# Expert stages of a two-layer mixture-of-experts backbone: TensorE's work in a written order, and weight tiles that hold two neighbouring rows per partition

## The chip, the cores and the metric

The kernel runs on one core of a Trainium2 chip, as one launch. Its metric is the device time of that launch in microseconds. A core has a matrix engine (TensorE, PE in the profile), a vector engine (VectorE, DVE), a scalar engine (ScalarE, ACT), a general engine (GpSimd, POOL), an engine that here only issues transfers (SyncE, SP) and 16 DMA engines that move data between the device memory and the on-chip memory. All work on their own and wait for one another through semaphores.

## What is computed

Two layers work on 512 latent tokens and 256 context tokens of 1024 features, all in fp32. Each layer is a sequence mixer (an mLSTM in layer 0, a retention in layer 1) followed by a mixture of 16 experts, in which every expert chooses its own tokens. The mixture is the part that the change is about:

```python
def expert_choice_ffn(h, router, w_gate, w_up, w_down):
    bn, t, _ = h.shape
    cap = CAPACITY_FACTOR * t // N_EXPERTS          # 64 latent or 32 context tokens
    aff = jax.nn.softmax(h @ router, axis=-1)
    gate, idx = lax.top_k(jnp.swapaxes(aff, 1, 2), cap)
    xs = h[bidx, idx]
    hid = jax.nn.silu(einsum('becd,edf->becf', xs, w_gate)) * einsum('becd,edf->becf', xs, w_up)
    y = einsum('becf,efd->becd', hid, w_down) * gate[..., None]
    return jnp.zeros_like(h).at[bidx, idx].add(y)
...
for i in range(DEPTH):                              # 2 layers
    ...                                             # mixer, added to x (and to ctx in layer 0)
    h_lat = modulate(rmsnorm(x, norm_ffn_g[i]), mod_l[3], mod_l[4])
    x = x + mod_l[5] * expert_choice_ffn(h_lat, moe_router[i], moe_w_gate[i], moe_w_up[i], moe_w_down[i])
    if not last:                                    # layer 0 alone: the context stream too
        h_ctx = modulate(rmsnorm(ctx, norm_ffn_g[i]), mod_c[3], mod_c[4])
        ctx = ctx + mod_c[5] * expert_choice_ffn(h_ctx, moe_router[i], ...)
return rmsnorm(x, final_norm_g)
```

Every expert has three matrices of 1024 x 1024 fp32 (4.19 MB each), so a layer reads 16 x 12.58 MB = 201.3 MB of expert weights, each used once.

## The kernel before

**Weights.** `load` (L1165) fetches the matrices on SP's queue in tiles of 1.05 MB: 128 partitions x 2 x 1024 fp32, that is 256 rows of a matrix, of which partition p holds row p and row p + 128. An expert has 12 tiles, in the order that `order` gives: four of gate, four of up, four of down. The tiles rotate through a fixed number of slots on the chip (`slot`; about 19 in layer 0 and 14 in layer 1). A load is issued when the last matmul that read its slot is done, so SP often stands and waits for PE.

**Layer 0.** An expert of the loop at the end of `moe` has 64 latent tokens (LAT in the code) and 32 context tokens (CTX). `prod` (L1276, its matmuls at L1282) makes a product: for each of 8 tiles of 128 features it puts the tokens as the stationary operand into a group of columns of PE and moves a piece of a weight row past them. The products are `gl` (gate, latent: 32 matmul records in the trace, 64 x 512), `ul` (up, latent), `cg` (gate and then up of the context: 64 records of 32 x 256 each, two halves of one accumulator) and `y` (down, of both streams, in the accumulators y0 and y1). Between them stand transposes: `xp` (L1243) turns the gathered token rows of the next expert into the stationary form, `hp` (L1433) does so with the hidden rows. ACT makes silu of the gate product (`hid`, L1425), DVE multiplies it by the up product (L1427), ACT copies `hp` into `hT` (L1435). DVE also scales the transposed tokens (`xs`, L1253 and L1255). GpSimd gathers tokens and adds results through indirect transfers.

**Layer 1.** Only latent tokens are left. Tokens are picked by matmuls with a 0/1 matrix for two experts at a time: `pick` (DVE, L1221), `xr` (8 matmuls of 128 x 512 for each half of the features, L1235), `rows` (ACT copy, L1238), `xp` (L1247), `xs`. After every odd expert the results of two experts are put back into the latent rows: `put_back` splits them into `bh` and `bl` (L296, L297), 16 matmuls `back` (L1313) spread them over the tokens, and DVE adds each 128 x 512 piece into x (L1316). The piece's accumulator `back` has two buffers. Expert 15 has a path of its own (`final_gain`, `finish`), in an order written by hand.

**What sets the order.** Outside that last expert a scheduler of the compiler orders the instructions of all engines, PE's too: the code gives the dependences, and the scheduler moves pieces of `gl`, `cg`, `ul`, `y`, `xr` and `back` between one another. Within `with tc.manual_schedule(engines=PE)` PE's instructions stand as the code is written.

## Time and profile before

| | |
|---|---|
| median of 3 runs | 1977.88 us (1977.67 to 1979.93) |
| the profiled execution | 1974.15 us |
| its span in the profile | 1972.4 us |
| mean granted clock of PE | 0.986 of full speed |
| PE busy | 1850.9 us, 94% of the span |
| DVE, ACT, POOL busy | 37%, 22%, 14% of the span |
| read from device memory | 544.13 MB |

The span is the time from the first to the last instruction in the profile; 1.75 us of the execution lie around it. The steady part of the expert loop of layer 0 lies between 533 and 1017 us, that of layer 1 between 1499 and 1921 us; together they are 906 us, 46% of the span. The rest are the two mixers, the routing, and the ends of the stages.

### The profile page before, as it was taken

The page shows a single profiled execution, that of the slowest core. Times are in us where ns is not written, and L with a number is a line of the kernel's source. Part 1 is how long each engine was busy: PE and PEld are TensorE (multiplying, and loading weights), DVE is VectorE, ACT ScalarE, POOL GpSimd, SP SyncE. Part 2 cuts the span into 40 slices and gives each one's busy share as a digit, 9 for nine tenths or more (in the row PEclk, how much of TensorE's full clock was granted, in tenths as well). Part 3 has the DMA queues.
Part 4 walks back from the last instruction along what each step waited for, and adds up shares of the span by engine and source line. Part 5 has one row for each costly group of instructions (what it writes and reads, how often), then busy time and mean ns, then how long its engine had stood idle before and what let it go on. Part 6 is the DMA issues. An engine that isn't in the chain of part 4 may idle for free. (4 is left out here: it accounts for less than half of the span.)

```text
span 1972.4 us, 27775 instructions
## 1 busy us (share of the span) xinstructions
PE 1850.9 (94%) x11091; PEld 1012.6 (51%) x11091; DVE 730.2 (37%) x1739; ACT 426.8 (22%) x839; POOL 279.8 (14%) x340
## 2 busy tenths in 40 slices
PE   7999988999999999999998999999979999989997
PEld 2765766787344443333334777788754333333332
DVE  3544567546111110110104677355551322222223
ACT  3532355432000000000004522322411000000001
POOL 1111133301211121120011124144000000000001
PEclk9999999999999999999999999999979999999999
DMA  8567776764999999999984588354559999999992
GB/s 285 205 209 268 253 207 196 230 228 144 333 393 375 391 383 384 383 382 393 401 319 126 182 279 276 112 173 150 208 208 395 415 416 414 415 414 414 416 413 86
DMA packets 218258, 585.42 MB, mean 297 GB/s; under 512 B 17674, under 2 KB 69618, under 8 KB 213010
## 3 DMA queue, kind: packets, MB, share of 16 engines
q1 hardware_dynamic: 209840, 570.72, 77.6%
q0 software_dynamic: 6912, 12.71, 3.2%
q8 instruction: 88, 1.44, 0.3%
q10 hardware_dynamic: 1378, 0.23, 0.1%
q14 instruction: 40, 0.33, 0.0%
HBM read 544.13 MB, written 39.47 MB: 296 GB/s over the span
## 5 line engine op out<-in xcount | busy, mean ns | idle before, releaser
L1282 PE MATMUL y<-wslot,hT 128*32 128x256 f32 (+1 forms) x2016 | 291.1, 488 | 9.8 <-ACT hT L1435 9.6
L1282 PE MATMUL gl<-wslot,xs 128*64 128x512 f32 x1024 | 260.3, 610 | 0.8 <-DVE xs L1255 0.8
L1282 PE MATMUL ul<-wslot,xs 128*64 128x512 f32 x1024 | 239.3, 596 | 0.0
L290 PE MATMUL acc<-whi,hT_hi 128*128 128x512 f32 x544 | 223.2, 411 | 4.8 <-ACT hT_hi L360 3.1
L291 PE MATMUL acc<-wlo,hT_hi 128*128 128x512 f32 x544 | 217.6, 400 | 0.3 <-POOL wlo L297 0.3
L292 PE MATMUL acc<-whi,hT_lo 128*128 128x512 f32 x544 | 217.3, 399 | 0.2 <-DVE hT_lo L361 0.2
L1427 DVE TENSOR_TENSOR hid<-hid,ul 128x512 f32<-128x512 f32 x32 | 22.0, 688 | 463.5 <-PE ul L1282 463.5
L1282 PEld LDWEIGHTS y<-wslot,hT 128*32 128x32 f32 (+1 forms) x2016 | 100.2, 123 | 178.1 <-issue 137.3
L1282 PEld LDWEIGHTS ul<-wslot,xs 128*64 128x64 f32 x1024 | 72.2, 137 | 140.8 <-issue 136.2
L1282 PEld LDWEIGHTS gl<-wslot,xs 128*64 128x64 f32 x1024 | 69.4, 138 | 135.5 <-issue 131.1
L290 PEld LDWEIGHTS acc<-whi,hT_hi 128*128 128x128 f32 x544 | 102.8, 189 | 39.4 <-issue 9.8
L1282 PE MATMUL cg<-wslot,xs 128*32 128x256 f32 x1920 | 118.9, 382 | 0.5 <-ACT hid L1425 0.5
L292 PEld LDWEIGHTS acc<-whi,hT_lo 128*128 128x128 f32 x544 | 102.8, 189 | 28.5 <-issue 4.9
L291 PEld LDWEIGHTS acc<-wlo,hT_hi 128*128 128x128 f32 x544 | 103.2, 190 | 23.7 <-issue 2.4
L1425 ACT ACTIVATE hid<-gl 128x512 f32<-128x512 f32 x32 | 19.1, 597 | 439.6 <-PE gl L1282 439.6
L297 DVE TENSOR_TENSOR wlo<-wslot,whi 128x512 fp32r<-128x512 f32 x108 | 80.6, 762 | 56.1 <-ACT whi L296 55.8
L1282 PEld LDWEIGHTS cg<-wslot,xs 128*32 128x32 f32 x1920 | 56.5, 109 | 84.1 <-issue 51.1
L296 ACT ACTIVATE whi<-wslot 128x512 fp32r<-128x512 f32 x112 | 69.4, 630 | 99.2 <-PE acc L292 98.2
L1435 ACT ACTIVATE hT<-hp 128x512 f32<-128x512 f32 (+1 forms) x48 | 23.7, 524 | 297.4 <-PE hp L1433 297.4
L1387 POOL TENSOR_TENSOR wslot<-x,wslot 128x512 f32<-128x512 f32 x4 | 5.0, 1271 | 493.2 <-DVE x L1330 491.6
L290 PE MATMUL po<-woh,yh 128*128 128x512 f32 x160 | 64.5, 403 | 3.2 <-ACT yh L923 3.2
L1449 DVE SCALAR_TENSOR_TENSOR o<-y,gcol,M 128x512 f32<-128x512 f32 (+1 forms) x32 | 19.8, 617 | 125.8 <-PE y L1282 125.8
(440 smaller groups left out, 2449.9 us busy)
## 6 DMA issues: line engine op xcount, KB each, us to landing
wslot<-in_moe_w_up_dram SPq DMA_DIRECT2D x128, 1024.0 KB
wslot<-in_moe_w_gate_dram SPq DMA_DIRECT2D x128, 1024.0 KB
wslot<-in_moe_w_down_dram SPq DMA_DIRECT2D x124, 1024.0 KB
wslot<-in_ada_w_dram SPq DMA_DIRECT2D x40, 1024.0 KB
wslot<-in_ret_w_in_dram SPq DMA_DIRECT2D x16, 1024.0 KB
wslot<-in_mlstm_w_in_dram SPq DMA_DIRECT2D x12, 1024.0 KB
wslot<-in_ada_w_dram SPq DMA_DIRECT2D x16, 512.0 KB
E<-rows_d SPq DMA_DIRECT2D x24, 256.0 KB
```

Source lines behind the costliest of these rows:

```text
L290: nc.tensor.matmul(o, lh, rh, start=first, stop=False)
L291: nc.tensor.matmul(o, lh, rl, start=False, stop=False)
L292: nc.tensor.matmul(o, ll, rh, start=False, stop=last)
L296: nc.scalar.activation(wh, w, AF.Copy)
L297: eng.tensor_tensor(wl, w, wh.bitcast(F32), op=OP.subtract)
L1282: mm = nc.tensor.matmul(o[cw * q:cw * q + cw, :], stat(k), w(k)[:, qn * n:(qn + 1) * n], start=(k == 0), stop=(k == 7), tile_position=(0, ...
L1387: nc.gpsimd.tensor_tensor(O[:, lo], R.X[t][:, lo], fg[:, lo], op=OP.mult)
L1425: nc.scalar.activation(HID[v], o, AF.Silu)
L1427: nc.vector.tensor_tensor(HID[v], HID[v], o, op=OP.mult)
L1435: LATE["act"] = nc.scalar.activation(HT[v], p, AF.Copy)
L1449: LATE["dve"] = nc.vector.scalar_tensor_tensor(r, o, TOP[v][2][:, e:e + 1], M5[v], op0=OP.mult, op1=OP.mult)
```

## The change

Three things are changed together.

1. A weight tile holds two neighbouring rows of the matrix in each partition (rows 2p and 2p + 1 of its 256), which lie in one piece of 8 KB in device memory; before, they were two pieces of 4 KB. The down matrix of the very last expert comes in pieces of 2 KB as before. Sizes, number and order of the loads stay.
2. So the feature that a partition holds is another, and whatever meets a weight tile on the feature axis is brought into that order: either the transposes of it read every second column, or the operation that writes it writes its elements in pairs 128 apart (`paired`, `pairs_of`). This touches the modulation vectors (a new tile `vcp`, filled by three loads `VP`), the router, the normalised rows, and `hid`, which ACT and DVE now write in that pattern in every expert.
3. PE's order in the expert loops is written by hand (`ordered(engines=PE_ONLY)`): layer 0 for experts 1 to 14, layer 1 for experts 0 to 14. `prep`, `put_back` and `turn` are cut into pieces for that (`pick_rows`, `row_columns`, `add_back`, `turn_first`, `turn_last`).

```diff
@@ load @@
                                       dram_ap(w_down, off + (b % 2 * 512 + j * 256) * D + b // 2 * 512,
-                                              [[D, 128], [128 * D, 2], [1, 512]]))
+                                              [[2 * D, 128], [D, 2], [1, 512]]))
             else:
-                nc.sync.dma_start(w, dram_ap((w_gate, w_up, w_down)[m], off + b * 256 * D,
-                                             [[D, 128], [128 * D, 2], [1, D]]))
+                nc.sync.dma_start(w.rearrange("p a c -> p (a c)"),
+                                  dram_ap((w_gate, w_up, w_down)[m], off + b * 256 * D, [[2 * D, 128], [1, 2 * D]]))
@@ the order of features @@
+    def paired(row):
+        return row.rearrange("p (b j q) -> p b q j", j=2, q=128)
+    def pairs_of(row):
+        return row.rearrange("p (b q j) -> p b j q", j=2, q=128)
...
+        for r0, src, off, n in ((0, norm_ffn_g, 0, 8), (8, ada_b, 2 * D, 16), (24, ada_b, 8 * D, 16)):
+            nc.scalar.dma_start(VP[r0:r0 + n, :], dram_ap(src, off, [[256, n], [1, 256]]))
...
-                nc.tensor.transpose(p[:, kk, :], XM[n][:, (b * 4 + kk) * 128:(b * 4 + kk + 1) * 128], ident)
+                c0 = b * 512 + kk // 2 * 256
+                nc.tensor.transpose(p[:, kk, :], XM[n][:, c0 + kk % 2:c0 + 256:2], ident)
...
             if l:
-                nc.scalar.activation(R.XH[n], XM[n], AF.Copy, scale=rs)
-                nc.vector.scalar_tensor_tensor(R.XL[n], XM[n], rs, R.XH[n].bitcast(F32), op0=OP.mult, op1=OP.subtract)
+                xm = XM[n].rearrange("p (b q j) -> p b q j", j=2, q=128)
+                nc.scalar.activation(paired(R.XH[n]), xm, AF.Copy, scale=rs)
+                for j in range(2):
+                    jl, jh = [a.rearrange("p (b j q) -> p b j q", j=2, q=128)[:, :, j] for a in (R.XL[n], R.XH[n].bitcast(F32))]
+                    nc.vector.scalar_tensor_tensor(jl, XM[n][:, j::2].rearrange("p (b q) -> p b q", q=128), rs, jh,
+                                                   op0=OP.mult, op1=OP.subtract)
...
-                nc.scalar.activation(HID[v], o, AF.Silu)
+                nc.scalar.activation(paired(HID[v]), o.rearrange("p (b q j) -> p b q j", j=2, q=128), AF.Silu)
             else:
-                nc.vector.tensor_tensor(HID[v], HID[v], o, op=OP.mult)
+                h = paired(HID[v])
+                nc.vector.tensor_tensor(h, h, o.rearrange("p (b q j) -> p b q j", j=2, q=128), op=OP.mult)
@@ the loop over the experts @@
+            if e == 1 - l:
+                region.enter_context(ordered(engines=PE_ONLY))
+            if two and e == NE - 1:
+                region.close()
+            if l and e < NE - 1:
+                if e:
+                    gate_up(LAT, xs, 0, wg)
+                    if e % 2:
+                        pick_rows(e + 1, 0)
+                    else:
+                        add_back(0, 1)
+                    gate_up(LAT, xs, 1, wu)
+                W = weights(e + 1)
+                if e % 2:
+                    xs = sbx.tile([128, 8, NT], F32, name="xs", bufs=1)
+                    row_columns(0, xs)
+                    pick_rows(e + 1, 1)
+                    turn_first(LAT)
+                    row_columns(1, xs)
+                    turn_last(LAT)
+                else:
+                    add_back(2)
+                    if e + 2 < NE:
+                        select(e + 2)
+                    turn_first(LAT)
+                    add_back(3)
+                    turn_last(LAT)
+                down(LAT, e, wd)
+                continue
             if two and e not in (0, NE - 1):
                 gate_up(LAT, xs, 0, wg)
                 gate_up(CTX, xs, 0, wg)
+                gate_up(CTX, xs, 1, wu)
                 gate_up(LAT, xs, 1, wu)
-                gate_up(CTX, xs, 1, wu)
+                W = weights(e + 1)
+                xn = sbx.tile([128, 8, NT], F32, name="xs", bufs=2)
+                if e + 2 < NE:
+                    for v in streams:
+                        R.gather(e + 2, v)
+                prep(e + 1, xn, streams if e + 2 < NE else (LAT,))
+                turn(CTX)
+                turn(LAT)
+                down(CTX, e, wd)
+                down(LAT, e, wd)
+                xs = xn
+                continue
```

How the order of PE's instructions changes is shown by rows of the two programs: the line, the operation, out<-in by the program's names, the tile, and how many follow one another. Each matmul of `prod` that stands here gives two records in the trace.

PE in layer 0, before, in the later experts of the loop: the end of one expert's `ul` and `cg`, its transposes `hp` (first latent, then context), the next expert's `xp`, and the two products `y` in alternation.

```order
L1282 MATMUL ul<-wslot,xs 64x512 x4
L1282 MATMUL cg<-wslot,xs 32x256 x8
L1433 MATMUL hp<-ident,hid_7165 128x128 x4
L1433 MATMUL hp<-ident,hid_7200 128x128 x2
L1243 MATMUL xp<-ident,xg 128x96 x4
L1282 MATMUL y_7311<-wslot,hT_7304 64x512 x4
L1282 MATMUL y_7331<-wslot,hT_7309 32x256 x5
L1282 MATMUL y_7311<-wslot,hT_7304 64x512 x4
L1282 MATMUL y_7331<-wslot,hT_7309 32x256 x10
```

PE in layer 0 with the change, one whole expert from its `gl` on stands behind the end of the expert before.

```order
L1259 MATMUL xp<-ident,xg 128x96 x8
L1478 MATMUL hp<-ident,hid_6774 128x128 x2
L1478 MATMUL hp<-ident,hid_6739 128x128 x4
L1317 MATMUL y_6885<-wslot,hT_6876 32x256 x32
L1317 MATMUL y_6921<-wslot,hT_6883 64x512 x16
L1317 MATMUL gl<-wslot,xs 64x512 x16
L1317 MATMUL cg<-wslot,xs 32x256 x64
L1317 MATMUL ul<-wslot,xs 64x512 x16
```

Each product is now one block, the two halves of `cg` follow one another ahead of `ul`, and `xp` and the context's `hp` stand between `ul` and the latent `hp`.

PE in layer 0, with the semaphores that it waits for, before, at an early expert: the second half of `cg` stands behind `ul`, and waits for ACT there.

```order
L1282 MATMUL ul<-wslot,xs 64x512 [waits DMAHW3_49]
L1282 MATMUL ul<-wslot,xs 64x512 x3
L1282 MATMUL cg<-wslot,xs 32x256 [waits Activation_49]
L1282 MATMUL cg<-wslot,xs 32x256 x31
L1243 MATMUL xp<-ident,xg 128x96 [waits DMASW6_49,DMASW0_49,PE_49]
```

The same place with the change: `cg`'s second half follows its first at once, with the wait for ACT (and for the first tile of the up matrix) between them.

```order
L1317 MATMUL gl<-wslot,xs 64x512 x3
L1317 MATMUL cg<-wslot,xs 32x256 x16
L1317 MATMUL cg<-wslot,xs 32x256 [waits DVE_49]
L1317 MATMUL cg<-wslot,xs 32x256 x15
L1317 MATMUL cg<-wslot,xs 32x256 [waits DMAHW2_49,Activation_49]
L1317 MATMUL cg<-wslot,xs 32x256 x7
```

PE in layer 1, before, behind the product `y` of an odd expert: the matmuls `back` of the put-back are spread over the next expert's `gl`.

```order
L1433 MATMUL hp<-ident,hid_12141 128x128 x4
L1282 MATMUL y_12234<-wslot,hT_12232 64x512 x16
L1282 MATMUL gl<-wslot,xs 64x512 x2
L1313 MATMUL back<-bh_12253,put_12257 128x512
L1313 MATMUL back<-bh_12259,put_12263 128x512
L1313 MATMUL back<-bl_12260,put_12263 128x512
L1282 MATMUL gl<-wslot,xs 64x512
L1313 MATMUL back<-bl_12254,put_12257 128x512
```

PE in layer 1 with the change, at the same place: all of `gl` comes first, then eight `back` (four stand here), then `ul`; eight more `back` follow behind `ul`.

```order
L1317 MATMUL y_12253<-wslot,hT_12251 64x512 x16
L1317 MATMUL gl<-wslot,xs 64x512 x16
L1351 MATMUL back<-bh_12272,put_12276 128x512
L1351 MATMUL back<-bl_12273,put_12276 128x512
L1351 MATMUL back<-bh_12278,put_12282 128x512
L1351 MATMUL back<-bl_12279,put_12282 128x512
```

The put-back's matmuls now start 16 matmuls later than `y`'s end, and one block of them is cut in two only by `ul`.

## Rows read from the trace of the kernel before

**Rows 1.** Windows: busy time of each engine, PE's clock, DMA share, GB/s, both expert loops.

```profile
533.00:1017.00 484.00, 482.05 (x4132) 185.76 (x4124) 63.20 (x163) 25.73 (x56) 64.02 (x49) 1.00 1.03 388
1499.00:1921.00 422.00, 390.21 (x1696) 142.70 (x1694) 105.77 (x169) 34.79 (x58) 0.00 (x0) 1.00 1.03 414
```

**Rows 2.** Waits of PE, 540 to 1025 us: total, times, longest; the only row.

```profile
PE y L1282 <- ACT hT L1435: 1.4, 5, 0.3
```

**Rows 3.** Waits of PE, 1500 to 1915 us: first and last of five rows.

```profile
PE hp L1433 <- DVE hid L1427: 10.3, 12, 0.9
...
PE xr L1235 <- DVE pick L1221: 1.0, 1, 1.0
```

**Rows 4.** Waits of SP's queue, 1500 to 1920 us: the largest row.

```profile
SPq L1177 <- PE gl L1282: 142.6, 55, 5.7
```

**Rows 5.** Timeline of ACT, layer 0: start, duration; experts 1, 2 and 14.

```profile
554.13 0.87 ACT L1435 ACTIVATE hT<-hp 128x512 f32<-128x512 f32 x2 [11.51 <-PE hp L1433]
588.50 0.87 ACT L1435 ACTIVATE hT<-hp 128x512 f32<-128x512 f32 x2 [11.51 <-PE hp L1433]
...
1016.32 0.87 ACT L1435 ACTIVATE hT<-hp 128x512 f32<-128x512 f32 x2 [11.71 <-PE hp L1433]
```

**Rows 6.** Timeline of PE, layer 0, an early expert: start, duration.

```profile
645.21 7.09 PE L1282 MATMUL ul<-wslot,xs 128*64 128x512 f32 x32
652.23 3.66 PE L1282 MATMUL cg<-wslot,xs 128*32 128x256 f32 x64
655.82 0.88 PE L1243 MATMUL xp<-ident,xg 96*128 96x96 f32 x8
656.54 1.05 PE L1433 MATMUL hp<-ident,hid 128*128 128x128 f32 x6
657.52 0.64 PE L1282 MATMUL gl<-wslot,xs 128*64 128x512 f32 x1
```

**Rows 7.** Timeline of PE, end of layer 0's loop.

```profile
1016.97 11.95 PE L1282 MATMUL y<-wslot,hT 128*64 128x512 f32 x96 [0.28 <-ACT hT L1435]
1028.85 7.09 PE L1282 MATMUL gl<-wslot,xs 128*64 128x512 f32 x32
...
1057.77 3.66 PE L1282 MATMUL cg<-wslot,xc 128*32 128x256 f32 x64 [0.51 <-ACT hid L1425]
```

**Rows 8.** Timeline of DVE behind the `ul` of rows 6.

```profile
652.42 0.69 DVE L1427 TENSOR_TENSOR hid<-hid,ul 128x512 f32<-128x512 f32 x1 [17.18 <-PE ul L1282]
...
656.41 0.62 DVE L1253 TENSOR_TENSOR xs<-xp,gsc 128x256 f32<-128x256 f32 x2
```

**Rows 9.** Timeline of PE, layer 1: `y` of experts 1, 3 and 13, and pieces between.

```profile
1521.94 7.04 PE L1282 MATMUL y<-wslot,hT 128*64 128x512 f32 x32
...
1578.05 7.09 PE L1282 MATMUL y<-wslot,hT 128*64 128x512 f32 x32 [0.75 <-ACT hT L1435]
...
1592.35 1.08 PE L1282 MATMUL gl<-wslot,xs 128*64 128x512 f32 x4
1593.36 0.50 PE L1313 MATMUL back<-bh,put 128*128 128x512 f32 x1
...
1594.48 1.08 PE L1282 MATMUL gl<-wslot,xs 128*64 128x512 f32 x4
...
1883.28 7.09 PE L1282 MATMUL y<-wslot,hT 128*64 128x512 f32 x32 [0.75 <-ACT hT L1435]
...
1921.61 1.89 PE L1282 MATMUL gl<-wslot,xs 128*64 128x512 f32 x8
```

**Rows 10.** DMA, 1520 to 1900 us: expert weights in pieces of 4 KB.

```profile
DMA packets 40813, 157.52 MB, mean 415 GB/s; under 512 B 2399, under 2 KB 2399, under 8 KB 40797
```

**Rows 11.** DMA, 1155.5 to 1158.5 us: weights of the modulation, in pieces of 8 KB.

```profile
DMA packets 172, 1.28 MB, mean 426 GB/s; under 512 B 16, under 2 KB 16, under 8 KB 16
```

**Rows 12.** Windows as in rows 1, where the last expert's loads run out.

```profile
1925.00:1930.00 5.00, 5.00 (x20) 1.32 (x16) 0.96 (x2) 0.00 (x0) 0.00 (x0) 1.00 0.72 270
```

**Rows 13.** Windows as in rows 1, ahead of layer 1's experts.

```profile
1460.00:1465.00 5.00, 2.42 (x11) 2.26 (x12) 2.43 (x11) 0.00 (x0) 0.64 (x2) 0.81 0.00 0
1465.00:1470.00 5.00, 5.00 (x20) 3.75 (x22) 0.41 (x1) 0.91 (x2) 0.00 (x0) 0.50 0.00 0
```

More of the change, by code (lines that the diff above doesn't have):

```diff
@@ L1227, in prep @@
             a, b = SPAN[parts[0]][0], SPAN[parts[-1]][1]
-            if l:
-                pick = select(e)
             for hh in range(2):
-                if l:
-                    p = mp.tile([128, 512], F32, name="xr", tag="tp", bufs=3)
-                    for t in range(4):
-                        for part in (R.XH, R.XL):
-                            nc.tensor.matmul(p, pick[:, t, :], part[t][:, hh * 512:hh * 512 + 512],
-                                             start=(t == 0 and part is R.XH), stop=(t == 3 and part is R.XL))
-                    rows_ = sb.tile([128, 512], F32, name="rows", tag="hT0", bufs=1)
-                    nc.scalar.activation(rows_, p, AF.Copy)
                 p = mp.tile([128, 4, NT], F32, name="xp", tag="tp", bufs=3)
@@ new lines, in prep, with modulated @@
+                    if LATE.get("hold"):
+                        behind([LATE["xp"]], LATE["hold"])
+                modulated(p, hh, xs, parts)
+        def modulated(p, hh, xs, parts):
+            s = slice(hh * 4, hh * 4 + 4)
+            for v in parts:
+                c0, c1 = SPAN[v]
+                n = c1 - c0
+                o = xs[:, s, c0:c1] if xs.shape[2] == NT else xs[:, s, :]
+                nc.vector.tensor_tensor(o, p[:, :, c0:c1], gsc[l][1][:, s, v:v + 1].to_broadcast([128, 4, n]),
+                                        op=OP.mult)
+                LATE["xs"] = nc.vector.tensor_tensor(o, o, modcol[l][:, 24 + hh * 4:28 + hh * 4, v:v + 1]
+                                                     .to_broadcast([128, 4, n]), op=OP.add)
@@ new lines, in moe, with pick_rows @@
+        ROWS = {}
+        def pick_rows(e, hh):
+            pick = select(e)
+            p = mp.tile([128, 512], F32, name="xr", tag="tp", bufs=3)
+            for t in range(4):
+                for part in (R.XH, R.XL):
+                    nc.tensor.matmul(p, pick[:, t, :], part[t][:, hh * 512:hh * 512 + 512],
+                                     start=(t == 0 and part is R.XH), stop=(t == 3 and part is R.XL))
+            ROWS[hh] = sb.tile([128, 512], F32, name="rows", tag="hT0", bufs=1)
+            nc.scalar.activation(ROWS[hh], p, AF.Copy)
@@ L1259, in prep_first, with row_columns @@
+        def row_columns(hh, xs):
+            p = mp.tile([128, 4, NT], F32, name="xp", tag="tp", bufs=3)
+            for kk in range(4):
+                nc.tensor.transpose(p[:, kk, :], ROWS[hh][:, kk * 128:(kk + 1) * 128], ident)
+            modulated(p, hh, xs, streams)
         def prep_first(xs, *groups):
@@ L1308, in put_back, with add_back @@
                 nc.vector.tensor_scalar(put[q], R.tok, R.pair[:, q, e // 2:e // 2 + 1], None, op0=OP.is_equal)
-            for t in range(4):
+        def add_back(*ts):
+            for t in ts if "put" in BACK else ():
                 for q in range(2):
                     p = mp.tile([128, 512], F32, name="back", bufs=2)
-                    for part in (hi, lo):
-                        nc.tensor.matmul(p, put[q][:, t * 128:(t + 1) * 128], part[q],
-                                         start=part is hi, stop=part is lo)
+                    for part in ("hi", "lo"):
+                        nc.tensor.matmul(p, BACK["put"][q][:, t * 128:(t + 1) * 128], BACK[part][q],
+                                         start=part == "hi", stop=part == "lo")
                     xq = R.X[t][:, q * 512:(q + 1) * 512]
@@ L1492, in moe @@
                 gate_up(CTX, xs, 0, wg)
+                gate_up(CTX, xs, 1, wu)
                 gate_up(LAT, xs, 1, wu)
-                gate_up(CTX, xs, 1, wu)
-            elif l and e == NE - 1:
-                with tc.manual_schedule(engines={mybir.EngineType.PE}):
-                    fg = final_gain()
-                    for what, w in enumerate((wg, wu)):
-                        for b in range(4):
-                            gate_up(LAT, xs, what, w, range(2 * b, 2 * b + 2))
-                            next(BACK["steps"], None)
-                    turn(LAT)
-                    finish(fg)
-            elif not l or e:
-                gate_up(LAT, xs, 0, wg)
-                gate_up(LAT, xs, 1, wu)
-            if e + 1 < NE:
-                W = weights(e + 1)
-                if two or e % 2:
-                    xn = sbx.tile([128, 8, NT], F32, name="xs", bufs=2 - l)
-            if two and e == 0:
+                W = weights(e + 1)
+                xn = sbx.tile([128, 8, NT], F32, name="xs", bufs=2)
[9 more added lines that the diff above has]
+                continue
+            if l:
+                fg = final_gain()
+                for what, w in enumerate((wg, wu)):
+                    for b in range(4):
+                        gate_up(LAT, xs, what, w, range(2 * b, 2 * b + 2))
+                        next(BACK["steps"], None)
+                turn(LAT)
+                finish(fg)
+                continue
+            gate_up(LAT, xs, 0, wg)
+            gate_up(LAT, xs, 1, wu)
+            if e == 0:
+                W = weights(e + 1)
+                xn = sbx.tile([128, 8, NT], F32, name="xs", bufs=2)
                 turn(LAT)
```

124 lines of the change are left out of this document (59 added, 65 removed).

## The prediction

> **What bounds the kernel now.** I read the windows of the two expert loops first, since the change's new order and its new loads act there. The reader is to see that both resources are full. In layer 0 PE is busy 482.05 of 484 us, in layer 1 390.21 of 422, at full clock, and the DMA share is 1.03 in both, 388 and 414 GB/s [rows 1]. So the next view is the list of PE's waits: which of the two sets the pace? In layer 0 PE waits 1.4 us in all [rows 2]; in layer 1 the idle 31.8 us (422 less 390.21) are waits for DVE and ACT [rows 3], and no row names a DMA. SP's queue, on the other hand, waits for PE, 142.6 us for `gl` alone [rows 4]: a load is issued when PE frees its slot. PE sets the pace, and the loads run ahead of it by all slots.
>
> How far ahead shows at the end. The share of 0.72 in the last window puts the end of the loads at 1925 + 5 x 0.72/1.03 = 1928.5 us [rows 12]. When the first gate tile of expert 15 has landed, 11 tiles of 1.05 MB are still to come, 27.8 us at 415 GB/s [rows 10], so it landed at about 1900.7; PE takes it up at 1921.61 [rows 9]. PE is 21 us behind the loads. That is the most that a faster PE can win in layer 1 with the loads as they are: an expert pair of PE takes (1883.28 - 1578.05)/5 = 61.05 us [rows 9], and 24 tiles of 1.049 MB at 415 GB/s take 60.7.
>
> **Layer 0, the order.** The period of an expert is read from ACT's copies `hT`: 588.50 - 554.13 = 34.37 us early, and (1016.32 - 554.13)/13 = 35.55 in the mean over 13 periods [rows 5]; the later ones are longer, where the products alternate in small pieces. With the change each product is one block, and a period is a sum of blocks, each from its start to the next one's: three of the latent kind (`gl`, `ul`, `y`) at 652.23 - 645.21 = 7.02; three of the context kind (two halves of `cg`, `y`) at 655.82 - 652.23 = 3.59; `xp` 0.72; `hp` 0.98 [rows 6]. That is 33.53 us.
>
> Two waits come on top. The second half of `cg` waits for ACT's silu of the first: 0.51 us where the same sequence stands before, in expert 15 [rows 7]; what hid it was `ul`, and behind it in PE's queue stand `ul` and all else. And the latent `hp` now comes 0.72 + 0.33 = 1.05 us behind `ul`. The product that it needs is ready 0.19 + 0.69 = 0.88 us behind `ul` [rows 6, 8], but its accumulator is one of three that two `xp` and one `hp` already hold, and the first is free only when DVE, which does the product first, has read it: 0.88 + 0.6 = 1.5 us [rows 8]. I take 0.5; 0 if the accumulator is free sooner, and 1.0 if it waits for the second read. Together 34.5 us, bounds 33.5 to 35.5. Thirteen periods are 448.5, against 462.19: -13.7. The last `y`, 11.88 us in alternation [rows 7], becomes 10.61: -1.3. Layer 0: **-15.0 us** (-28 to -2).
>
> Do the loads keep up? An expert's 12.58 MB in 34.5 us are 365 GB/s, and the loop moved 388 in all, of which the weights were 12.58 MB in 35.55 us, 354, and 34 the gathers and sums. That asks for 399 GB/s; 388 x 426/415 = 398 are there by the rates of the next part. The two are level, and the cover is PE's lag: about as long as layer 1's by the same count of slots. I cost it at nothing; without it an expert takes 34.6.
>
> **Layer 1, the loads.** A piece of a load becomes 8 KB. The nearest row before is the modulation's weights, whose pieces are 8 KB: 426 GB/s over 3 us [rows 11], against 415 for pieces of 4 KB [rows 10], 2.6% more. The stretch is short; below, the gain could be nothing, above it I see no row. From 1476, where the loads are in full flow, to 1928.5 that is 452.5 x 2.6% = 11.7 us.
>
> **Layer 1, the order.** PE alone, per pair of experts: six latent blocks at 7.02 = 42.1; 16 `xr` and 16 `back`, four of which take 1594.48 - 1593.36 = 1.12 us with their change of shape [rows 9], 8.5 in the larger blocks (estimate); 16 transposes 2.1 by rows 6: 52.7. Waits: `y` for `hT` 0.75 us [rows 9], which stays in odd experts less an `xp`, 0.4; `back` for DVE, which empties each accumulator in about the 0.69 us of a 128 x 512 operation [rows 8] where PE fills one in 0.5: 0.8 for the block of eight; 1.1 for the copies of `rows` and the rest. What goes is the wait of `back` for `bh` and of `hp` for `hid` (0.9 at most [rows 3]): `gl` or `xr` and `back` now stand ahead of them. **55 us per pair**, bounds 53 and 57.4 (61.05 less 2.7 of waits and 0.9 of changes of shape). From `y` of expert 1 at 1521.94, six pairs and 33.6 to the end of `y` of expert 14 put expert 15 at 1885.5 by PE alone, or 1900 at 57.4.
>
> By the loads alone the end is 1928.5 - 11.7 = 1916.8, and the first gate tile of expert 15 has landed 27.1 us (11 tiles at 426) before, 1889.7; with 1.2 us for half a tile's slack, 1890.9. The later limit holds: PE starts expert 15 at 1890.9 instead of 1921.61, **-30.7 us**, and from there 50.8 us to the span's end stay as they are: their PE chain is unchanged, and a tile of the loads (2.5 us) comes faster than PE uses one. So layer 1 becomes bound by the loads, at 59 us a pair. The pieces' waits in this loop then cost nothing up to about 4 us a pair; the loads hide them.
>
> **The rest.** Three more loads of vectors, strided transposes, a split DVE operation in layer 1's rows: 0.5 us, 0 to 4. Hidden behind the weights at the start they cost nothing; without that cover, the upper bound. The two rows per partition are no work of their own.
>
> Sum: -15.0 - 30.7 + 0.5 = -45.2. The profiled execution, 1974.15 with 1.75 us around its span, becomes 1929.0; the median of the runs is 3.7 above the profiled one, so **1932.7 us**.
>
> **The rivals.**
>
> (a) The long pieces bring little. A stretch of 3 us proves no rate. With no gain the first gate tile of expert 15 is there at 1901.9, and the sum is -34; with half of it -40: 1938 to 1944, **1941**. The Trainium skill ("DMA: Bandwidth & Descriptors", section "Why small descriptors are slow (HBM only)") gives a fixed overhead of about 3 cycles per packet beside 32 bytes per cycle: an estimate from it is 131 against 129.5 cycles for 4 KB, 1.2%, half of what rows 11 and 10 say; by it alone the sum would be near -39. Chance 0.15.
>
> (b) The pair pattern slows ACT and DVE. Their hid operations step 512 bytes at every second element; no row before has that pattern. Bound from above: they take twice as long, DVE's product 1.38 instead of 0.69 [rows 8], and the wait of `cg` for the silu, 0.51 [rows 7], doubles too. In layer 0 1.2 us x 14 = 16.8 are on PE's path, and its gain is gone; in layer 1 PE alone comes to about 56.4 a pair, and expert 15 starts at 1894.6, 3.7 us behind the loads' limit. Sum -15.0 + 16.8 - 30.7 + 3.7 + 0.5 = -24.7, **1953 us**. The lower bound is nothing, and I take that: the nearest row is the same operation in unit steps, 0.69. The Trainium skill ("SBUF — State Buffer", section "Door 1: The DMA port swizzle (why `[64,N]` ≈ `[32,N]`)") speaks against the change here: lines are 16 bytes, and an access that goes to a new line pays. No run here shows it yet. Chance 0.12.
>
> (c) The loads already set the pace in both loops, and the order is worth nothing. For it: the share of 1.03 [rows 1]. Then 2.6% of 484 and of 452 us are won, 24 us: **1954 us**. Against it: PE waits for no DMA [rows 2, 3]. Chance 0.07.
>
> (d) Slower: PE's clock falls in layer 1. With the loads as the bound PE stands still some 4 us in 59, in short waits at the tiles. One stretch shows what idling does: behind a stretch at 2.42 us busy of 5, five full microseconds ran at a clock of 0.50, which is 1.2 GHz, [rows 13]. Expert 15 starts six pairs and 33.6 us behind `y` of expert 1, 363.6 us at full clock; the whole gain of layer 0 and the time of before are used up when that takes 1921.61 - 1521.94 + 14.5 = 414 us: a mean clock of 0.88, and 0.87 for 0.2% slower. At 0.81 it takes 449, and the kernel some 35 us longer, **2013 us**. Against it: before, PE idled 7.5% in that loop at a clock of 1.00 [rows 1], and each wait was below 1.5 us. Chance 0.05.
>
> **How the numbers follow.** The forecast has 0.61, the rivals 0.39. A measurement of this kernel can tell about 0.2%, 4 us, from no change. The forecast and (a) to (c) all end faster, 0.95; 0.03 of that I give to no change, for several bad bounds that meet. So 0.92 faster, 0.03 the same, 0.05 slower. The forecast's own range is from its bounds, above all layer 0's -28 to -2 around -15: 1920 to 1946; its lowest microsecond, which needs no wait at all, I leave out. The range takes in (a) to (c): 1921 to 1956; what lies outside is (d) and some 0.1 of mishaps on both sides.
>
> **What would show it.** Right: copies `hT` 34.5 us apart in layer 0, all alike; waits of the second `cg` half for ACT near 0.5 us, 14 times, and of `hp` for DVE below 1 us; pieces of 8 KB at 426 GB/s; in layer 1 waits of PE released by the loads in the later experts, where there were none, `y` of odd experts 59 us apart there, and the first `gl` of expert 15 30 to 31 us nearer to layer 1's start. Wrong: `hid` operations longer than 0.69 us on DVE (b); a rate near 415 (a); a clock below 1.00 in the loop (d); no wait for a load at all, which would mean that PE alone takes over 59 us a pair and that my sum of its blocks fails.

## The result, and the profile after

The change takes **1946.73 us** (median of 4 runs, 1945.22 to 1948.51) against 1977.78 us, a ratio of 0.9847 with a 95% interval of 0.9827 to 0.9867: 31 us faster, where 45 were forecast. The range (1921 to 1956) holds the time, and the sign is right.

The page of the profile after: span, PE's line, and the chain that ended last by engine.

```profile
span 1946.7 us, 27790 instructions
...
PE 1816.5 (93%) x11093; PEld 1025.2 (53%) x11093; DVE 741.9 (38%) x1745; ACT 457.5 (23%) x839; POOL 277.6 (14%) x340
...
PE 21%; DMA 12%; DVE 3%; POOL 1%; issue 1%; ACT 1%; POOLq 0%; SPq 0%; DVEq 0%; ACTq 0%
```

The reader is to see two things: DMA, which was 1% of the chain before, is 12% of it; and ACT is busy 30.7 us more (457.5 against the 426.8 of before), though it has the same 839 instructions. The first was forecast, the second was not.

**Layer 0.** ACT's copies `hT` of the latent stream, after, for experts 1 and 14 (they answer to [rows 5]), and PE's timeline over one expert ([rows 6]):

```profile
562.19 0.60 ACT L1483 ACTIVATE hT<-hp 128x512 f32<-128x512 f32 x1 [0.74 <-PE hp L1478]
...
1013.25 0.60 ACT L1483 ACTIVATE hT<-hp 128x512 f32<-128x512 f32 x1 [0.81 <-PE hp L1478]
```

```profile
676.67 7.04 PE L1317 MATMUL gl<-wslot,xs 128*64 128x512 f32 x32
683.64 3.66 PE L1317 MATMUL cg<-wslot,xs 128*32 128x256 f32 x64
688.03 3.66 PE L1317 MATMUL cg<-wslot,xs 128*32 128x256 f32 x64 [0.73 <-ACT hid L1463]
691.62 7.09 PE L1317 MATMUL ul<-wslot,xs 128*64 128x512 f32 x32
698.64 0.88 PE L1259 MATMUL xp<-ident,xg 96*128 96x96 f32 x8
...
700.27 0.66 PE L1478 MATMUL hp<-ident,hid 128*128 128x128 f32 x4 [0.53 <-ACT hT L1483]
```

Thirteen periods are 451.06 us, 34.70 each; 34.5 were forecast. Two waits stand in the expert, in the places where they were forecast: `cg`'s second half for silu (0.73 instead of 0.51) and the latent `hp` (0.53; 0.5 was forecast). What ends the second is another operation than the one forecast: the row names ACT's copy `hT` of the context, not DVE.

**Layer 1.** PE's waits after, 1470 to 1890 us (total, times, longest), the first three of six rows, and `y` of experts 1 and 13 and the first `gl` of expert 15 on PE's timeline ([rows 9]):

```profile
PE gl L1317 <- DMA wslot<-in_moe_w_gate_dram: 6.2, 13, 0.7
PE y L1317 <- ACT hT L1483: 5.9, 8, 0.7
PE back L1351 <- DVE x L1354: 2.2, 7, 0.3
```

```profile
1522.87 7.09 PE L1317 MATMUL y<-wslot,hT 128*64 128x512 f32 x32 [0.75 <-ACT hT L1483]
...
1859.57 7.09 PE L1317 MATMUL y<-wslot,hT 128*64 128x512 f32 x32 [0.75 <-ACT hT L1483]
...
1895.66 1.94 PE L1317 MATMUL gl<-wslot,xs 128*64 128x512 f32 x8
```

Waits for loads have appeared. The chain that ended last, followed back from the end of the program, runs over the loads in the later part of this loop: of its rows in order of time (start, duration) these are the first and the last of the loads there.

```profile
1653.82 19.75 DMA wslot<-in_moe_w_up_dram
...
1853.05 19.66 DMA wslot<-in_moe_w_gate_dram
```

PE itself feels them later. ACT's copies `hT` of the odd experts 7 to 13:

```profile
1685.56 0.60 ACT L1483 ACTIVATE hT<-hp 128x512 f32<-128x512 f32 x1 [0.81 <-PE xp L1291]
...
1739.99 0.60 ACT L1483 ACTIVATE hT<-hp 128x512 f32<-128x512 f32 x1 [0.81 <-PE xp L1291]
...
1798.92 0.60 ACT L1483 ACTIVATE hT<-hp 128x512 f32<-128x512 f32 x1 [0.81 <-PE xp L1291]
...
1858.92 0.60 ACT L1483 ACTIVATE hT<-hp 128x512 f32<-128x512 f32 x1 [0.81 <-PE xp L1291]
```

Up to about 1740 us PE goes its own pace, 54.4 us from one odd expert to the next, and none of its waits is for a load; then the loads set the pace, 58.9 and 60.0 us. From `y` of expert 1 to `gl` of expert 15 it is 372.8 us, 399.7 before; the forecast had 1890.9 - 1521.94 = 369.0.

**What was not forecast.** Of the groups of instructions by line (count, busy us, mean ns), the four largest that became longer:

```profile
L1463 ACT ACTIVATE hid<-gl 128x512 f32<-128x512 f32 x32 | 35.4, 1106 | 400.5 <-PE gl L1317 400.5
L994 ACT ACTIVATE fxt<-xm,rs 128x1024 f32<-128x1024 f32 x6 | 12.9, 2143 | 0.2 <-POOL rs L985 0.2
L988 ACT ACTIVATE xh<-x,rs 128x1024 fp32r<-128x1024 f32 x4 | 8.5, 2128 | 0.4 <-POOL rs L985 0.4
L1466 DVE TENSOR_TENSOR hid<-hid,ul 128x512 f32<-128x512 f32 x32 | 34.8, 1089 | 271.1 <-PE ul L1317 271.1
```

They were 597, 1155, 1147 and 688 ns before. All four write in the pair pattern; `fxt` and `xh` are the normalised rows of layer 0 and layer 1, XT and XH in the code. Where no other PE work hides `hid`, PE now waits longer for it, and in this profile its clock is low behind the wait: expert 0 of layer 0 on PE's timeline, and the window of its `y`.

```profile
512.89 0.66 PE L1478 MATMUL hp<-ident,hid 128*128 128x128 f32 x4 [1.23 <-DVE hid L1466]
514.23 8.78 PE L1317 MATMUL y<-wslot,hT 128*64 128x512 f32 x32 [0.69 <-ACT hT L1483]
```

```profile
514.00:517.00 3.00, 2.77 (x8) 0.84 (x10) 0.00 (x0) 0.18 (x1) 0.00 (x0) 0.63 1.04 429
```

A `y` that takes 7.09 us at full clock took 8.78, at a mean granted clock of 0.63 in its first three microseconds (part of them at the lower of the two levels, 1.2 GHz, part at 2.4), behind waits of 1.23 and 0.69 us. The same 8.78 stands at expert 15 of layer 0, behind a wait of 1.23 us, and at expert 0 of layer 1, behind waits of 0.82 and 0.69 us.

### The profile page after: what moved, and what is told of

Its sections match the earlier page's. It is cut to its first block, busy times and chain, and to the rows that moved or that the text cites. A ratio compares the mean times of both kernels' runs of the same rounds, so it can differ in the third digit from the quotient of the medians.

```text
span 1946.7 us, 27790 instructions
## 1 busy us (share of the span) xinstructions
PE 1816.5 (93%) x11093; PEld 1025.2 (53%) x11093; DVE 741.9 (38%) x1745; ACT 457.5 (23%) x839; POOL 277.6 (14%) x340
## 5 line engine op out<-in xcount | busy, mean ns | idle before, releaser
L1317 PE MATMUL y<-wslot,hT 128*32 128x256 f32 (+1 forms) x2016 | 282.8, 492 | 7.4 <-ACT hT L1483 7.3
L1317 PE MATMUL gl<-wslot,xs 128*64 128x512 f32 x1024 | 235.8, 603 | 7.1 <-DMA wslot<-in_moe_w_gate_dram 6.2
L1317 PE MATMUL ul<-wslot,xs 128*64 128x512 f32 x1024 | 229.1, 596 | 1.0 <-DMA wslot<-in_moe_w_up_dram 1.0
L1466 DVE TENSOR_TENSOR hid<-hid,ul 128x512 f32<-128x512 f32 x32 | 34.8, 1089 | 271.1 <-PE ul L1317 271.1
L1463 ACT ACTIVATE hid<-gl 128x512 f32<-128x512 f32 x32 | 35.4, 1106 | 400.5 <-PE gl L1317 400.5
L1317 PE MATMUL cg<-wslot,xs 128*32 128x256 f32 x1920 | 109.8, 380 | 11.0 <-ACT hid L1463 10.2
L1466 DVE TENSOR_TENSOR hid<-hid,cg 128x256 f32<-128x256 f32 x16 | 9.8, 614 | 207.0 <-PE cg L1317 207.0
```

The lines of the kernel that those rows point to most:

```text
L1317: mm = nc.tensor.matmul(o[cw * q:cw * q + cw, :], stat(k), w(k)[:, qn * n:(qn + 1) * n], start=(k == 0), stop=(k == 7), tile_position=(0, ...
L1463: nc.scalar.activation(paired(HID[v]), o.rearrange("p (b q j) -> p b q j", j=2, q=128), AF.Silu)
L1466: nc.vector.tensor_tensor(h, h, o.rearrange("p (b q j) -> p b q j", j=2, q=128), op=OP.mult)
```

## The experiments

Two theories stood against each other. **A**: the pair pattern costs what is missing of the forecast. **B**: it is harmless, and what is missing lies in the mixers and the loads. All times are medians of five or six runs, but for one kernel with a single run. Four kernels each share a chip and its runs of the kernel before (1976.5, 1977.1 and 1976.2 us); across chips the ratios are the safer comparison.

**Order alone, and rows alone.** The first has the loads of before and every feature where it was, in the loop of the change; the second has the loads and features of the change, with the loop, `prep`, `put_back` and `turn` of before. Against the change, the first:

```diff
-                nc.sync.dma_start(w.rearrange("p a c -> p (a c)"),
-                                  dram_ap((w_gate, w_up, w_down)[m], off + b * 256 * D, [[2 * D, 128], [1, 2 * D]]))
+                nc.sync.dma_start(w, dram_ap((w_gate, w_up, w_down)[m], off + b * 256 * D,
+                                             [[D, 128], [128 * D, 2], [1, D]]))
...
-                nc.scalar.activation(paired(HID[v]), o.rearrange("p (b q j) -> p b q j", j=2, q=128), AF.Silu)
+                nc.scalar.activation(HID[v], o, AF.Silu)
```

and the second:

```diff
-            if e == 1 - l:
-                region.enter_context(ordered(engines=PE_ONLY))
...
             if two and e not in (0, NE - 1):
                 gate_up(LAT, xs, 0, wg)
                 gate_up(CTX, xs, 0, wg)
-                gate_up(CTX, xs, 1, wu)
                 gate_up(LAT, xs, 1, wu)
+                gate_up(CTX, xs, 1, wu)
```

> TensorE's written order alone, with the loads in pieces of 4 KB and every feature where it was. Theory A (the pair pattern of the second part costs what is missing from the forecast: ACT's and DVE's operations on hid, XT and XH are half as long again to twice as long, and the idling that this causes lowers the clock at the ends of the loops): hid back at 0.60 and 0.69 us, a period of 34.4 us in layer 0, no y block of 8.8 us; in layer 1 pairs of 54 us until the loads at 415 GB/s set the pace at 60.7, so the gain there is the 20 us of lag: about 1977.8 - 13 - 20 = 1945 us, as fast as the whole change. Theory B (the pattern is harmless, and what is missing is in the mixers and the loads): the same loops, but the 8 KB pieces are missing: about 10 us slower than the whole change, 1957 us.

> Rows of 8 KB and reordered features alone, with the scheduler's order of before. Theory A: TensorE sets the pace, so the faster loads are worth nothing, and the pattern costs: hp waits 1.23 instead of 0.86 us for hid in layer 1, 15 times, some 4 us where the clock falls behind longer idling, 4 to 6 us at the ends of the mixers: 1985 to 1992 us. Theory B: 1976 to 1979 us. That the loads were the bound all along (rival c of the prediction) would give some 1955 us.

Order alone: **1941.84 us**, 0.9823 (0.9804 to 0.9842). Rows alone: **1993.85 us**, 1.0080 (1.0060 to 1.0101), so one half of the change is a loss by itself, and the other half alone is at least as fast as the whole (0.9847, and 0.9831 when it was run again; the intervals overlap). Order alone has `hid` at 598 and 688 ns and 13 periods of 34.47 us. In rows alone no load is among PE's waits in layer 1, and the largest of them, 1490 to 1880 us, is longer than before ([rows 3]):

```profile
PE hp L1460 <- DVE hid L1453: 12.7, 11, 1.2
```

Both are nearer to A, which had 1945 and 1985 to 1992 us, than to B with 1957 and 1976 to 1979; the rows alone lose a little more than A put on them. Rival (c) falls too: the order, which it held for worthless, wins 34.6 us by itself, and the faster loads without it win nothing.

**Runs instead of pairs.** The same elements go to the same places, but in another order: two runs of 128, read with a step of 8 bytes and written contiguously.

```diff
     def paired(row):
-        return row.rearrange("p (b j q) -> p b q j", j=2, q=128)
+        return row.rearrange("p (b j q) -> p b j q", j=2, q=128)
...
-                nc.scalar.activation(paired(HID[v]), o.rearrange("p (b q j) -> p b q j", j=2, q=128), AF.Silu)
+                nc.scalar.activation(paired(HID[v]), o.rearrange("p (b q j) -> p b j q", j=2, q=128), AF.Silu)
```

> The whole change, with the same elements written to the same places, but in another order: two runs of 128 elements, read with a step of 8 bytes and written contiguously, instead of pairs 512 bytes apart. Theory A: hid at 0.60 to 0.65 us on ACT and 0.69 to 0.75 on DVE, XT and XH at 1.15 instead of 2.1 us; the wait of cg for silu 0.5 instead of 0.73 us, a period of 34.4 us, y of expert 0 and 15 at 7.1 instead of 8.8 us: 8 to 13 us faster than the change, 1934 to 1939 us. Theory B: no change in the total beyond 2 us, 1945 to 1949 us. If an 8-byte step costs as much as the pair, hid stays at 1.1 us.

**1937.11 us**, 0.9797 (0.9778 to 0.9815): 9.6 us below the change's first median, 7.4 below its second (1944.50, further on). Neither was run beside this kernel; its interval lies below that of the first (0.9827 to 0.9867) and just touches that of the second (0.9808 to 0.9853). `hid` is back at 598 and 687 ns, XT and XH at 1225 and 1218, the period at 34.47 us. Expert 0 of layer 0 on PE's timeline, and its window:

```profile
511.46 0.66 PE L1478 MATMUL hp<-ident,hid 128*128 128x128 f32 x4 [0.85 <-DVE hid L1466]
512.81 7.09 PE L1317 MATMUL y<-wslot,hT 128*64 128x512 f32 x32 [0.69 <-ACT hT L1483]
```

```profile
512.50:515.50 3.00, 2.69 (x14) 0.98 (x16) 0.00 (x0) 0.25 (x1) 0.00 (x0) 1.00 1.03 426
```

Here, behind a wait of 0.85 us, the clock is at 1.00. The wait of the latent `hp` in layer 0's period is still 0.53 us, although DVE's product is 0.4 us shorter. On the timeline of one expert, DVE's read of the first `xp` ends at 695.49, ACT's copy `hT` of the context at 695.74, and `hp` starts at 695.79:

```profile
694.88 0.61 DVE L1270 TENSOR_TENSOR xs<-xp,gsc 128x256 f32<-128x256 f32 x2
...
695.36 0.38 ACT L1483 ACTIVATE hT<-hp 128x256 f32<-128x256 f32 x1 [11.86 <-PE hp L1478]
...
695.79 0.66 PE L1478 MATMUL hp<-ident,hid 128*128 128x128 f32 x4 [0.53 <-ACT hT L1483]
```

Theory B falls, as far as it holds the pattern harmless.

**Which of the two, `hid` or the rows?** The change once more, and the change with runs in XT and XH alone.

```diff
     def paired(row):
-        return row.rearrange("p (b j q) -> p b q j", j=2, q=128)
+        return row.rearrange("p (b j q) -> p b j q", j=2, q=128)
...
-                h = paired(HID[v])
+                h = HID[v].rearrange("p (b j q) -> p b q j", j=2, q=128)
```

> The changed kernel itself, as a measure for the other three on the same chip: 1945 to 1949 us by its four runs.

> The changed kernel with two runs of 128 in XT and XH alone; hid is still written in pairs. It parts the 9.6 us that the runs are worth. By the trace hid costs: 13 x 0.2 in the periods of layer 0, 0.4 + 1.7 each at the experts 0 and 15 of layer 0 and expert 0 of layer 1 (the wait and the clock behind it), 0.4 or so at the two waits of cg, in all 9 to 10 us; XT and XH cost 0.9 us each on ACT, one or two of them on the path at each mixer's end, 2 to 4 us. So hid has the larger part: 1943 to 1946 us. If XT and XH are the cause instead (the mixers' ends): 1937 to 1940 us.

**1944.50 us** (0.9831, 0.9808 to 0.9853) and **1944.29 us** (0.9837, 0.9814 to 0.9861): the same. XT and XH are 0.9 us slower each in the change and it costs nothing that these runs can tell; what the pattern costs, it costs at `hid`.

The traces also show that the slow `y` is not there every time. Expert 0 of layer 1 on PE's timeline, of the change as first measured and of the kernel with `hid` alone in pairs:

```profile
1492.20 0.65 PE L1478 MATMUL hp<-ident,hid 128*128 128x128 f32 x4 [0.82 <-DVE hid L1466]
1493.54 8.78 PE L1317 MATMUL y<-wslot,hT 128*64 128x512 f32 x32 [0.69 <-ACT hT L1483]
```

```profile
1486.79 0.66 PE L1478 MATMUL hp<-ident,hid 128*128 128x128 f32 x4 [0.82 <-DVE hid L1466]
1488.13 7.09 PE L1317 MATMUL y<-wslot,hT 128*64 128x512 f32 x32 [0.69 <-ACT hT L1483]
```

The waits are the same, 0.82 and 0.69 us, and `y` takes 8.78 us in one and 7.09 in the other. Of the three places (experts 0 and 15 of layer 0, expert 0 of layer 1) all three are slow in the first trace of the change, two in its second, one in the kernel with `hid` in pairs, and none in any kernel whose latent `hid` is as short as before.

**What in the pattern is slow?** Other orders of elements in the same operations: in the latent `hid` an inner loop of two, 8 bytes apart; in the context's an inner loop of 64, 16 bytes apart; in XH runs of four elements, 2 KB apart.

```diff
+                if v == LAT:
+                    h = HID[v].rearrange("p (a j i) -> p a i j", i=2, j=2)
+                    nc.vector.tensor_tensor(h, h, o.rearrange("p (a i j) -> p a i j", i=2, j=2), op=OP.mult)
+                else:
+                    h = HID[v].rearrange("p (q j) -> p j q", j=4)
+                    nc.vector.tensor_tensor(h, h, o.rearrange("p (j q) -> p j q", j=4), op=OP.mult)
...
-                nc.scalar.activation(paired(R.XH[n]), xm, AF.Copy, scale=rs)
+                nc.scalar.activation(R.XH[n].rearrange("p (j a i) -> p a j i", j=2, i=4),
+                                     XM[n].rearrange("p (b a j i) -> p b a j i", b=4, j=2, i=4), AF.Copy, scale=rs)
```

> Only durations are of interest: the changed kernel with other orders of elements in the operations that the pair pattern slowed, so that hid and the rows XH hold their features in other places, and what is computed behind them is another sum. Latent hid: an inner loop of two elements 8 bytes apart, four elements (16 bytes) before it moves on. Context hid: an inner loop of 64 elements with a step of 16 bytes. XH on ACT: runs of four elements, then 2 KB on. Line theory (the rule of the Trainium skill: a line of 16 bytes wants two accesses in succession): latent hid as fast as in unit steps, 0.60 us on ACT and 0.69 on DVE; context hid as slow as in pairs, 0.61 us on both instead of 0.38 and 0.42; XH near 1.15 us. Loop theory (an inner loop of two elements is what costs): latent hid 1.1 us on both, context hid 0.38 and 0.42, XH between 1.15 and 2.1.

The groups by line of this kernel:

```profile
L1465 ACT ACTIVATE hid<-gl 128x512 f32<-128x512 f32 x32 | 19.1, 598 | 400.5 <-PE gl L1318 400.5
L1468 ACT ACTIVATE hid<-cg 128x256 f32<-128x256 f32 x16 | 9.9, 621 | 63.3 <-PE cg L1318 63.3
L988 ACT ACTIVATE xh<-x,rs 128x1024 fp32r<-128x1024 f32 x4 | 4.6, 1148 | 0.4 <-POOL rs L985 0.4
```

```profile
L1473 DVE TENSOR_TENSOR hid<-hid,ul 128x512 f32<-128x512 f32 x32 | 22.0, 688 | 272.4 <-PE ul L1318 272.4
L1476 DVE TENSOR_TENSOR hid<-hid,cg 128x256 f32<-128x256 f32 x16 | 10.1, 633 | 206.3 <-PE cg L1318 206.3
```

An inner loop of two is as fast as unit steps, and so are runs of 16 bytes with long jumps; an inner loop of 64 with a step of 16 bytes is as slow as the pairs (621 and 633 ns against 384 and 422). So it is not the short loop and not the distance: steps of 8 bytes are fast and steps of 16 slow, which fits that an access that leaves its 16 bytes at every element is what costs. The rule of the Trainium skill ("SBUF — State Buffer", section "Door 1: The DMA port swizzle (why `[64,N]` ≈ `[32,N]`)") on lines of 16 bytes says that, and the trace agrees.

The one run of this kernel took 1938.75 us. Its period in layer 0 is (1010.41 - 559.23)/13 = 34.71 us with a wait of 0.73 us for silu, as in the change, and its `y` at the three places takes 7.09. So the 0.2 us of each period come from the context's `hid` and the slow `y` goes with the latent one.

**The order in layer 0.** With runs, `cg`'s second half goes back behind `ul`, and the latent `hp` and `y` ahead of the context's:

```diff
                 gate_up(CTX, xs, 0, wg)
-                gate_up(CTX, xs, 1, wu)
                 gate_up(LAT, xs, 1, wu)
+                gate_up(CTX, xs, 1, wu)
...
                 prep(e + 1, xn, streams if e + 2 < NE else (LAT,))
-                turn(CTX)
                 turn(LAT)
-                down(CTX, e, wd)
+                turn(CTX)
                 down(LAT, e, wd)
+                down(CTX, e, wd)
```

> As the kernel with two runs of 128, and layer 0's order changed in two places: cg's second half behind ul again (so that ul hides silu and cg hides the product of hid and ul), and the latent hp and y ahead of the context's. Theory A and the sum of the prediction: no wait for silu, a period near 33.6 to 33.9 us, 13 x 0.6 = 8 us less in layer 0, passed on in full since the loads' stream of layer 1 starts when layer 0 ends: about 1927 us. If the loads bound layer 0 (12.58 MB at some 364 GB/s are 34.6 us) the gain ends when TensorE has used up its lag, and PE shows waits for loads there.

Then, with VP on another queue (below), the latent `hp` goes ahead of `xp` too:

```diff
+                turn(LAT)
                 prep(e + 1, xn, streams if e + 2 < NE else (LAT,))
-                turn(LAT)
                 turn(CTX)
```

> As the kernel with VP on GpSimd's queue, with the latent hp moved ahead of xp in layer 0, so that xp and the context's hp hide ACT's copy hT, for which y waits 0.3 us in each of 13 experts. Period 33.89 - 0.3 = 33.55 us, the sum of its blocks; 4 us faster, about 1922 us. If the fourth of three accumulators (the context's hp) then waits for hT, as hp waited for xs in the change, the wait comes back in another place and nothing is won.

The first: **1931.21 us** (0.9755, 0.9733 to 0.9778), 4 us above the 1927 expected, and 1931.59 on another chip; a period of 33.89 us, as expected; one kind of wait is left, `y` for `hT`, 0.3 us in each of 13 experts. The last: **1924.14 us** (0.9733, 0.9712 to 0.9754), the fastest kernel here, 20 to 23 us below the change's two medians. Its runs reach from 1917.0 to 1931.5 us, and the interval overlaps that of the kernel it is compared with, 1928.83; the period shows the gain without that doubt: (997.60 - 560.57)/13 = 33.62 us. One expert on its PE timeline:

```profile
690.89 3.66 PE L1317 MATMUL cg<-wslot,xs 128*32 128x256 f32 x64
694.48 0.66 PE L1478 MATMUL hp<-ident,hid 128*128 128x128 f32 x4
694.97 0.82 PE L1259 MATMUL xp<-ident,xg 96*128 96x96 f32 x8
695.88 0.44 PE L1478 MATMUL hp<-ident,hid 128*128 128x128 f32 x2
```

No wait is left in this expert, and a single one of 0.4 us between 540 and 1020 us: 33.53 was the prediction's sum of the blocks.

**The three loads VP.** They are issued on GpSimd's queue instead of ACT's, with the order of the first of the two.

```diff
-            nc.scalar.dma_start(VP[r0:r0 + n, :], dram_ap(src, off, [[256, n], [1, 256]]))
+            nc.gpsimd.dma_start(VP[r0:r0 + n, :], dram_ap(src, off, [[256, n], [1, 256]]))
```

> The kernel with two runs of 128 and cg's second half last, with the three loads VP issued on GpSimd's queue instead of ACT's at the start. Five profiles show the first large matmul of the first mixer 1.5 to 2.2 us later where the three loads are on ACT's queue (38.8 to 39.5 us from the start of the record, against 37.1 to 37.3). If ACT's three issues are the cause: 37 to 37.5, and the total 1 to 2 us below the 1931.2 of that kernel. If it is the second transpose and the three small transfers themselves, it stays at 39 and 1931.

> The kernel with two runs and cg last, as a measure on this chip: 1930 to 1932 us.

> The same with VP on GpSimd's queue. 5.7 us lay between the two in different jobs, of which the first large matmul showed 2.8. If the start is all, it is 1 to 3 us faster than the run of the same job without it; if the later start also lengthens the first mixer, 5 to 6 us.

**1925.54 us**, 5.7 below the 1931.21 that the same order took on another chip; on one chip **1928.83** (0.9763, 0.9748 to 0.9778) against **1931.59** (0.9772, 0.9751 to 0.9793): 2.8 us, less than the intervals tell apart. The trace shows the sign: ACT's first table load stands right behind the issues (ACTq) on ACT's timeline, first of the change and then of the kernel with VP on GpSimd's queue.

```profile
3.35 0.30 ACTq L103 DMA_DIRECT2D VP<-in_norm_ffn_g_dram  x1
3.69 1.16 ACTq L103 DMA_DIRECT2D VP<-in_ada_b_dram  x2
4.88 1.28 ACT L251 ACT_TABLE_LOAD   x1 [4.88 <-DMA V<-in_final_norm_g_dram]
```

```profile
3.31 1.28 ACT L251 ACT_TABLE_LOAD   x1 [3.31 <-DMA V<-in_norm_mix_g_dram]
```

The first large matmul of the mixer begins at 28.36 us in the change, 26.40 before, and 26.21 with VP on GpSimd's queue. Over all traces it is 27.28 to 28.36 us where VP is on ACT's queue, 26.02 to 26.78 where there is no VP, and 25.85 to 26.21 where VP is on GpSimd's: 1.4 us between the first two in the mean. How much of it reaches the end of the program is not shown.

**What the 8 KB are worth.** The order with `cg`'s second half behind `ul`, with pieces of 4 KB and every feature where it was before.

> What the 8 KB rows are worth once they cost nothing else: TensorE's written order with cg's second half behind ul, pieces of 4 KB, features as before. Against the kernel with order alone its layer 0 is 13 x 0.58 = 7.5 us shorter: 1941.8 - 7.5 = 1934 us. Against the same order with 8 KB rows, two runs and VP on GpSimd's queue it should be slower by the loads' term of layer 1, which is 435.99 - 427.39 = 8.6 us between the two kernels that differ in it: 8 to 9 us. If the rows are worth only the 4.7 us that the totals showed: 5 us.

**1934.57 us** (0.9796, 0.9778 to 0.9815), 5.7 above 1928.83 with the 8 KB, where 8 to 9 were expected from the loads' term alone. DMA in layer 1, 1530 to 1860 us, of order alone and of the change with runs:

```profile
DMA packets 35447, 136.81 MB, mean 415 GB/s; under 512 B 2085, under 2 KB 2085, under 8 KB 35431
```

```profile
DMA packets 19182, 139.79 MB, mean 424 GB/s; under 512 B 2130, under 2 KB 2130, under 8 KB 2130
```

The rate rises by 2.2%, and layer 1 from its first to its last `hT` by the two traces from 435.99 to 427.39 us, 8.6 less. The totals differ by 4.7 and 5.7: the same sign twice, though the intervals of each pair overlap or touch. The 3 to 4 us between them stay open. The kernels with 8 KB also carry the reordered features (XT and XH at 1225 and 1218 ns instead of 1155 and 1147, and the split DVE operation), and the stages ahead of the experts differ by more from profile to profile (the first `hT` of layer 0 stands at 509.54, 512.81 and 516.33 us in three profiles of kernels whose code up to there is the same).

## Why the prediction held, and what it missed

**What bounds the kernel.** Right. PE set the pace, with the loads a little ahead: the order alone uses up that lead and wins 34.6 us, and with the order of before PE waits for no load, fast or slow.

**Layer 0, -15.0.** From the first `cg` of expert 1 to `gl` of expert 15 it is 1023.59 - 544.82 = 478.8 us on PE's timeline after, and 1028.85 - 538.52 = 490.3 before: -11.6. The period was 0.2 us longer than forecast, by the silu wait of 0.73 instead of 0.51, which is the pair pattern; that is 2.6 of the 3.4 us. The blocks are at 7.02 and 3.59, as taken, and both waits went by order in the later kernels. The size of the second wait was luck: the forecast had `hp` wait for DVE's read of an `xp`, which the product delays. With the product 0.4 us shorter that read ended 0.30 us ahead of `hp`, and the wait stayed at 0.53 us; `hp` started 0.05 us behind the end of ACT's copy of the context. Why it needs that copy is not shown.

**Layer 1, -30.7.** The mechanism is right: PE alone at 54.4 us a pair (55 forecast; (1631.10 - 1522.22)/2 between the copies `hT`), then, from about 1740 us, the loads' pace of 59 to 60 (59 forecast). The size is -26.9. The term that was mis-sized is the loads' rate: 2.6% from a stretch of 3 us, 2.2% measured (415 to 424 GB/s), and 8.6 us of the 11.7 in layer 1. That is between the forecast and rival (a).

**The pair pattern, at nothing.** This is the step that failed: "the lower bound is nothing, and I take that". Writing in pairs made ACT's operations 1.85 times and DVE's 1.6 times as long, and cost 7 to 10 us. Rival (b) had the mechanism, with the rule that speaks for it, but not the place: it put 16.8 us on the periods of layer 0, where DVE's longer product turned out hidden behind `xp` and the wait of `hp`, and 13 x 0.2 us were lost. The rest went at the experts where nothing hides `hid`: 0.38 us more of waiting at three places, and 1.7 us of a slower `y` at those of them where the clock was low, three, two and one in the three traces with this order and `hid` in pairs.

**The rest, +0.5.** Too low. Between the two profiles the span fell by 25.7 us and the two loops by 38.5, so all else grew by 12.8. The medians fell by 31.05, and so 5.4 of these 12.8 belong to the choice of the two profiled executions. The start alone is 2 us later in them (28.36 against 26.40), since three issues on ACT's queue stood ahead of its first work, which I had as hidden behind the weights.

Together, the forecast was 14.1 us too fast: 3.4 in layer 0's loop (2.6 of them the pattern), 3.8 in layer 1's (3 of them the loads' rate), and 6.9 in the rest. The three places with a slow `y` (6.2 us in this profile) and the start (1.4 to 2) are as much as that rest, but this last part is an estimate: the stages ahead of the experts differ by several us from profile to profile. The rival on the slower side, (d), didn't come: from 1499 to 1890 us the mean granted clock was 1.00, with waits of at most 0.75 us; a low clock showed only at expert 0, ahead of that stretch.

## What to carry to other kernels

A reordering that is "free" because an operation runs anyway is free only if that operation still finds two elements of the same 16 bytes in succession: write it as two long runs with a small step, not as pairs far apart. When two resources are level, as PE and the loads here, first take out PE's own stalls: that uses up its lag behind the loads, and only then is a faster load worth anything. And look for the places in a steady loop's first and last turn where nothing hides a longer operation; of the 32 experts' turns here three carried up to 6.2 us of a loss of 7 to 10.

## What the runs showed of the hardware

ACT and DVE in fp32 ran as fast as in unit steps when they read the accumulators with a step of 8 bytes (598 and 687 ns for 128 x 512) and with an inner loop of two (598 and 688); ACT also in runs of 16 bytes 2 KB apart (1148 ns for 128 x 1024). ACT's read of the normalised rows with a step of 8 bytes cost 6% (1225 ns against 1155). Both took 1.5 to 1.85 times as long as soon as every element lay outside the 16 bytes of the one before (1106 and 1089 ns in pairs, 621 and 633 ns for 128 x 256 with a step of 16 bytes). Behind waits of PE of 0.85 and 0.69 us, one soon behind the other, its granted clock was 1.00 in every trace; behind 1.23 and 0.69 us at the same place, expert 0 of layer 0, it was 0.63 to 0.66 over the next three microseconds. The length of the waits alone doesn't decide it: behind 0.82 and 0.69 us at expert 0 of layer 1 the same `y` took 8.78 us in two traces and 7.09 in a third. Pieces of 8 KB moved 424 GB/s where pieces of 4 KB moved 415, in streams of 330 us.
